# A gathered running sum times a matrix, on one core: gathers that convert to 16 bits as they land, in place of a cast on ScalarE

## The chip, the cores and the metric

The kernel runs on one core of a Trainium2 chip. The metric is the device time of one execution in microseconds (us). Three executions of the kernel before gave 450.98, 449.62 and 450.46 us, so the median is 450.46 us. One more execution was taken with the hardware profiler, and it is the one that the profile shows.

The core has five engines with a queue of instructions each: TensorE (PE in the profile, with its weight loads as PEld), VectorE (DVE), ScalarE (ACT), GpSimd (POOL) and SyncE (SP). They wait for one another through semaphores. Transfers between the chip's memory (DRAM) and the on-chip memory run on 16 DMA engines; here SyncE issues the stores and GpSimd the gathers.

## The reference

```python
B, S, N, D = 16, 4096, 2048, 512       # x: [B, S, D] float32, indices: [B, N] sorted, w: [D, D]
gathered = x[b_idx, indices, :].copy()  # [B, N, D]
cs = np.cumsum(gathered, axis=1)        # running sum over the N gathered rows
return np.matmul(cs, w).astype(np.float32)
```

Each of 16 batches picks 2048 of its 4096 rows of 512 floats, sums them up from the first to each row, and multiplies every running sum by one 512 x 512 matrix. 67 MB are read and 67 MB written.

## The kernel before, in words

The 32,768 gathered rows are cut into 256 tiles of 128 rows, 16 tiles to a batch; two neighbouring tiles make a pair (`R = 2`). Each tile goes through six steps.

1. **Gather** (GpSimd, L136): one indirect DMA fetches 128 rows of 2 KB, one per partition, into a tile of `g32`, a ring of 8 pairs in float32. From the 17th tile on, a gather waits on `s_c` until the tile that stood in its place in the ring has been cast.
2. **Cast** (ScalarE, L150): a copy from `g32` to `g16`, a ring of 8 pairs in float16. It waits for its gather (`s_g`).
3. **Sums** (TensorE, L162): four matmuls against a triangle of ones (`ut`, or `uq` in the first and last two pairs), which give the running sums within the tile, already transposed, in `pa` (four tiles of PSUM).
4. **Carry** (VectorE, L194; L181 in the first tile of a batch): adds the last sum of the tile before and writes float16 to `cst` (a ring of four pairs). Each carry waits for the sums (`s_a`) and for the carry before (`s_d`).
5. **Projection** (TensorE, L206): four matmuls of 512 columns against `w16` into `pb` (four tiles of PSUM). The two tiles of a pair are interleaved row by row, so a projection waits until both carries of its pair are done.
6. **Drain** (ScalarE, L218): a copy from `pb` to `ob`, four buffers of four tiles. SyncE stores 1 MB from each when its four drains are done (L236); the first eight pairs and the last four are stored one by one.

The order on each queue is written out by hand. On TensorE a list (L343 to L351) puts the sums of a tile `LEAD = 2` tiles ahead of the projections, so that the queue reads sums of tile u + 2, projection of tile u, and so on; a projection also needs a free place in `pb` (`s_e`, the drain of the tile four before), and sums need a free place in `pa` (`s_d`, the carry of the tile four before). On ScalarE the queue reads cast of tile u + 4, drain of tile u (`FAR = 4`). GpSimd's queue holds nothing but the 256 gathers after a short setup. TensorE, VectorE and ScalarE run the middle of the program as loops with 16 tiles to a pass.

`Lane.need` (L21) is the helper that emits a wait, and leaves it out where the engine has already waited for as much.

Of the kernel before, what the change touches and what calls it, by code (L numbers as in the profile page):

```python
# [7 lines left out]
P = 128  # L8
FP32 = mybir.dt.float32
FP16 = mybir.dt.float16  # L10
# [23 lines left out]
def kernel(  # L34
# [7 lines left out]
    nc = tc.nc  # L42

    B, S, D = x.shape
    N = indices.shape[1]
    R = 2
    Q = P // R
    DC = D // P
    NT = N // P
    T = B * NT  # L50
# [2 lines left out]
    KI = T // P  # L53
    FIRST = 2 * R
    NG = 16
    LEAD = 2
    FAR = 4
    NH = 8
    NA = 4
    NB = 4  # L60
    NC = 4
    W = 2
    NO = 4
    U = NT
    V = max(U, W * R * NO)
    assert U == NT == NG == W * R * NO and V % U == 0 and V % (W * R * NO) == 0 and T % V == 0 and U % NG == 0 and U % NA == 0 and U % (R * NC) == 0 and U % NB == 0
    assert D == 512 and N % (R * P) == 0 and T % P == 0

    x_flat = x.rearrange("b s d -> (b s) d")
# [1 line left out]
    const = ctx.enter_context(tc.tile_pool(name="const", bufs=1))  # L71
# [8 lines left out]
    ut = const.tile([P, R, Q], FP16)  # L80
    uq = const.tile([P, P], FP16)
    ident = const.tile([P, P], FP32)
    zeros = const.tile([P, D], FP16)
    spare = const.tile([P, 1], FP16)
    g32 = [const.tile([P, R, D], FP32, name=f"g32_{i}") for i in range(NG // R)]
    g16 = [const.tile([P, R, D], FP16, name=f"g16_{i}") for i in range(NH)]
    cst = [const.tile([P, DC, R, P], FP16, name=f"cst{i}") for i in range(NC)]
    ob = [const.tile([P, W, R, D], FP32, name=f"ob{i}") for i in range(NO)]
    pa = [ps.tile([P, DC, R, Q], FP32, name=f"pa{i}") for i in range(NA)]
# [4 lines left out]
    def sem(name):  # L94
        return tc.alloc_semaphore(name)

    s_z, s_ut, s_wc, s_if, s_pt, s_prep, s_c = (
        sem(f"s_{n}") for n in ("z", "ut", "wc", "if", "pt", "prep", "c")
    )
# [2 lines left out]
    s_idx = [sem(f"s_idx{k}") for k in range(KI)]  # L102
    s_f = [sem(f"s_f{i}") for i in range(NO)]
    s_ol = sem("s_ol")
    s_g = [sem(f"s_g{i}") for i in range(NG)]
    s_o = [sem(f"s_o{i}") for i in range(NO)]
    s_a = sem("s_a")
    s_d = sem("s_d")
    s_b = sem("s_b")
    s_e = sem("s_e")  # L110

    pool, pe, dve, act, sp = (
        Lane(e) for e in (nc.gpsimd, nc.tensor, nc.vector, nc.scalar, nc.sync)
    )

    casts = []
    done = 0
    for u in range(T):
        far = 2 if u < R else 3 if u < U // 2 or T - 1 - u < R * R else FAR
        casts.append(range(done, max(done, min(u + far + 1, T))))  # L120
        done = max(done, min(u + far + 1, T))

    for u in range(2 * U, T - 2 * U):
        assert casts[u] == range(u + FAR, u + FAR + 1)

    def gather(t):
        g, r = divmod(t, R)
        if t >= NG:
            pool.need(s_c, R * (g + 1) - NG)
        if t < FIRST:  # L130
            pool.need(s_first[g], 16)
            ap = idx_first[:, t, 0:1]
        else:
            pool.need(s_prep, t // P + 1)
            ap = idxg[:, t // P, t % P : t % P + 1]
        nc.gpsimd.indirect_dma_start(  # L136
            out=g32[g % (NG // R)][:, r, :],
            out_offset=None,
            in_=x_flat,
            in_offset=bass.IndirectOffsetOnAxis(ap=ap, axis=0),  # L140
            element_offset=(t // NT) * S * D,
        ).then_inc(s_g[t % NG], 16)


    PLAIN = (0, 1, G - 2, G - 1)

    def cast(t, first=None):
        g, r = divmod(t, R)
        act.need(s_g[t % NG], 16 * (t // NG + 1), first)
        nc.scalar.copy(  # L150
            out=g16[g % NH][:, r, :], in_=g32[g % (NG // R)][:, r, :]
        ).then_inc(s_c, 1)

    def sums(t, u, first=None):
        g, r = divmod(t, R)
        tiles = None if first is None else R * first
        pe.need(s_c, t + 1, tiles)
        pe.need(s_d, t - NA + 1, tiles)
        for c in range(DC):
            if c == 1 and u is not None:  # L160
                pe.need(s_e, u - NB + 1, tiles)
            mm = nc.tensor.matmul(  # L162
                out=pa[t % NA][:, c],
                lhsT=g16[g % NH][:, r, c * P : (c + 1) * P],
                rhs=uq[:] if first is None and g in PLAIN else ut[:],
                start=(c == 0),
                stop=(c == DC - 1),
            )
        mm.then_inc(s_a, 1)
# [28 lines left out]
    def project(u, t, first=None):  # L198
        g, j = divmod(u, R)
        tiles = None if first is None else R * first  # L200
        pe.need(s_e, u - NB + 1, tiles)
        pe.need(s_d, u + 1 if first is None and g in PLAIN else R * (g + 1), tiles)
        for c in range(DC):
            if c == 2 and t is not None:
                pe.need(s_d, t - NA + 1, tiles)
            mm = nc.tensor.matmul(  # L206
                out=pb[u % NB][:],
                lhsT=cst[g % NC][:, c, j, :],
                rhs=w16[:, c, :],
                start=(c == 0),  # L210
                stop=(c == DC - 1),
            )
        mm.then_inc(s_b, 1)

    def drain(u, first=None):
        g, j = divmod(u, R)
        act.need(s_b, u + 1, first)
        nc.scalar.copy(out=ob[g // W % NO][:, g % W, j], in_=pb[u % NB][:]).then_inc(s_e, 1)  # L218
# [22 lines left out]
    with nc.allow_non_contiguous_dma(reason="a few indices, one per partition"):  # L241
        for k, eng in enumerate((nc.sync, nc.scalar)):
            t = k * R
            eng.dma_start(
                out=idx_first[:, t : t + R, :],
                in_=indices[0, t * P : (t + R) * P]
# [4 lines left out]
    for k in range(KI):  # L251
        nc.sync.dma_start(
            out=idx64[:, k, :], in_=idx_rows[k * P : (k + 1) * P, :]
# [10 lines left out]
    for i in range(G // W - NO, G // W - 2):  # L264
# [8 lines left out]
        out=ident[:],  # L273
        in_=ident[:],
# [7 lines left out]
        out=ut[:],  # L282
        in_=ut[:],
# [9 lines left out]
        out=uq[:],  # L293
        in_=uq[:],
# [6 lines left out]
    for t in range(T):  # L301
        gather(t)
# [15 lines left out]
    for k in range(KI):  # L318
# [3 lines left out]
            out=pb[k % NB][:, :P], in_=idxf[:, k, :], identity=ident[:]  # L322
# [20 lines left out]
    order = []  # L343
    done = 0
    for u in range(T):
        lead = 1 if min(u, T - 1 - u) < R * R else min(LEAD, 2 + (u + 4) // 16, 2 + (T - 1 - u) // 15)
        first = u if u // R in PLAIN else u // R * R + R - 1
# [4 lines left out]

    head = order.index((False, 2 * U - 1)) + 1
    tail = order.index((False, T - 2 * U - 1)) + 1
    step = 2 * U
    for i in range(head + step, tail):
        assert order[i] == (order[i - step][0], order[i - step][1] + U)

    def run(i, first=None):
        is_sums, t = order[i]  # L360
        after = next((v for k, v in order[i + 1 :] if k != is_sums), None)
        if first is not None:
            t -= 2 * U
            after -= 2 * U
        if is_sums:
            sums(t, after, first)
        else:
            pe.need(s_wc, DC)
            project(t, after, first)

    for i in range(head):
        run(i)
    with nc.tensor.Fori(2 * U // R, (T - 2 * U) // R, U // R) as first:
        pe.new_pass()
        for i in range(head, head + step):
            run(i, first)
    for i in range(tail, len(order)):
        run(i)
# [7 lines left out]
    def step(u, first=None):  # L386
        if u % (W * R) == 0:
            i, slot = divmod(u // (W * R), NO)
            if first is None and i == 1:
                act.need(s_f[slot], 16 * (W - 1 + (slot == 0) * (R - 1)))  # L390
            act.need(s_o[slot], 16 * i, first)
        for t in casts[u if first is None else 2 * U + u]:
            cast(t if first is None else t - 2 * U, first)
        drain(u, first)


    for u in range(2 * U):
        step(u)
    with nc.scalar.Fori(2 * U, T - 2 * U, V) as first:
        act.new_pass()  # L400
        for u in range(V):
            step(u, first)
    for u in range(T - 2 * U, T):
        step(u)
# [30 lines left out]
```

## Time and profile before

| what | value |
|---|---|
| median of three executions | 450.46 us |
| the profiled execution, its own time | 447.37 us |
| its span, from the first to the last instruction | 445.6 us |
| TensorE busy | 324.6 us |
| ScalarE busy | 278.2 us, of it casts 159.8 us and drains 150.6 us, which overlap a little |
| GpSimd busy | 244.3 us in 266 instructions, 256 of them gathers |
| VectorE busy | 178.9 us |
| moved by the DMA engines | 135.69 MB, mean 304 GB/s |

Times are microseconds unless marked ns. "Busy" is the time in which an engine had an instruction at work. A wait is put down to the instruction that released it; "remote" stands where the profile knows none, and "issue" is time in which the engine waited for nothing that the profile shows. Matmuls are pipelined and their ends are modelled, so the end of a matmul in the record is not the moment at which its result was announced. In the timeline, each row is the start, the length, the engine, the line and what was done, and in brackets how long the engine had been idle and what released it.

### The profile page before, as it was taken

Reading aid. Unit: us, or ns where it says so; the run is one execution under the profiler, and the core shown is the slowest. Engines: PE = TensorE matmul, PEld = TensorE weight load, DVE = VectorE, ACT = ScalarE, POOL = GpSimd, SP = SyncE. Lnnn points to the kernel's source line nnn. Section 1 sums busy time; section 2 is a strip of 40 time slices with the busy share of each in tenths; the row PEclk is TensorE's granted clock in tenths of the full one; section 3 lists DMA queues with packets and bytes.
Section 4 is the critical chain, followed back from the end, with each engine's and each line's share of the span. In section 5 each row is a group of like instructions: output and inputs, shape, how many; then the busy total and the mean of one; then the engine's idle time right before and its main releaser. Section 6 shows DMA issues by size and latency. Waiting matters only on the chain.

```text
span 445.6 us, 6369 instructions
## 1 busy us (share of the span) xinstructions
PE 324.6 (73%) x2066; PEld 168.1 (38%) x2066; DVE 178.9 (40%) x263; ACT 278.2 (62%) x516; POOL 244.3 (55%) x266
## 2 busy tenths in 40 slices
PE   7508777777778856968669677777688677777795
PEld 3203343344334433434335333343344333333452
DVE  2104343434334334444344434344434444334562
ACT  4206575667666656767567656666766666566794
POOL 6754555555565555656556555565564555555500
PEclk9757898989898999898997999898996999998999
DMA  7866878988998998899998999888998898998976
GB/s 228 258 197 209 313 267 303 346 300 326 325 330 307 313 335 311 300 348 317 323 326 276 320 301 338 306 317 316 342 324 305 311 313 308 322 314 311 333 282 257
DMA packets 39947, 135.69 MB, mean 304 GB/s; under 512 B 5888, under 2 KB 6144, under 8 KB 39936
## 3 DMA queue, kind: packets, MB, share of 16 engines
q0 software_dynamic: 20480, 67.13, 45.3%
q1 hardware_dynamic: 18896, 67.90, 41.3%
q10 hardware_dynamic: 560, 0.53, 0.4%
q8 instruction: 5, 0.08, 0.1%
q14 instruction: 6, 0.05, 0.0%
HBM read 68.42 MB, written 67.11 MB: 304 GB/s over the span
## 4 chain that ended last, share of the span: by engine, by line
PE 73%; DVE 10%; another core or an unknown queue 7%; issue 5%; ACT 1%; DMA 1%; POOL 0%; DVEq 0%; SPq 0%
PE pb L206 51%; PE pa L162 22%; DVE cst L194 10%; DMA g<-in_x_dram,idx_first 1%; ACT g L150 1%; ACT ob L218 1%; DMA idx_first<-in_indices_dram 0%; POOL g L136 0%; DVE cst L181 0%; DVEq L26 0%; DVEq L333 0%; SPq L430 0%; SPq L92 0%
## 5 line engine op out<-in xcount | busy, mean ns | idle before, releaser
L206 PE MATMUL pb<-w,cst 128*128 128x512 f16 x1024 | 284.7, 404 | 99.9 <-DVE cst L194 91.0
L136 POOL DMA_INDIRECT g<-in_x_dram,idxg x252 | 238.8, 948 | 175.1 <-ACT g L150 105.5
L194 DVE TENSOR_TENSOR cst<-pa,cst 128x512 f16<-128x512 f32 x240 | 166.1, 692 | 239.9 <-PE pa L162 168.8
L218 ACT COPY ob<-pb 128x512 f32<-128x512 f32 x256 | 150.6, 588 | 157.2 <-PE pb L206 94.2
L150 ACT CAST g<-g 128x512 f16<-128x512 f32 x256 | 159.8, 625 | 0.5 <-DMA g<-in_x_dram,idx_first 0.4
L206 PEld LDWEIGHTS pb<-w,cst 128*128 128x128 f16 x1024 | 91.6, 102 | 180.2 <-DVE cst L194 100.1
L162 PE MATMUL pa<-ut,g 128*128 128x128 f16 x992 | 100.9, 227 | 13.8 <-issue 12.6
L162 PEld LDWEIGHTS pa<-ut,g 128*128 128x128 f16 x992 | 79.4, 102 | 83.1 <-issue 30.7
L181 DVE CAST cst<-pa 128x512 f16<-128x512 f32 x16 | 11.0, 690 | 14.4 <-PE pa L162 9.1
L309 PE MATMUL pb<-zeros 128*128 128x512 f16 x16 | 7.2, 632 | 1.5 <-DVE zeros L313 1.5
L136 POOL DMA_INDIRECT g<-in_x_dram,idx_first x4 | 4.0, 1003 | 1.6 <-issue 0.9
L309 PEld LDWEIGHTS pb<-zeros 128*128 128x128 f16 x16 | 2.3, 150 | 4.8 <-issue 3.3
L162 PEld LDWEIGHTS pa<-uq,g 128*128 128x128 f16 x32 | 2.7, 111 | 2.3 <-ACT g L150 0.6
L162 PE MATMUL pa<-uq,g 128*128 128x128 f16 x32 | 3.4, 243 | 0.1
L385 ACT CAST w<-w 128x512 f16<-128x512 f32 x2 | 1.1, 618 | 2.9 <-DMA w<-in_w_dram 2.9
L382 ACT ACT_TABLE_LOAD x1 | 1.3, 1283 | 2.5 <-issue 2.5
L316 DVE CAST idxf<-idx 128x128 f32<-128x128 uint32 x2 | 0.5, 227 | 4.5 <-DMA idx<-in_indices_dram 4.5
L321 PE MATMUL pb<-ident,idxf 128*128 128x128 f32 x2 | 0.9, 449 | 0.7 <-DVE idxf L316 0.7
L321 PEld LDWEIGHTS pb<-ident,idxf 128*128 128x128 f32 x2 | 0.4, 207 | 1.6 <-DVE idxf L316 1.4
L330 DVE CAST w<-w 128x512 f16<-128x512 f32 x2 | 0.8, 428 | 0.3 <-DMA w<-in_w_dram 0.3
L313 DVE MEMSET zeros<- 128x256 uint32 x1 | 0.3, 272 | 1.1 <-SPq L92 1.1
L327 DVE CAST idxg<-pb 128x128 uint32<-128x128 f32 x2 | 0.6, 288 | 0.4 <-PE pb L321 0.4
(11 smaller groups left out, 2.1 us busy)
## 6 DMA issues: line engine op xcount, KB each, us to landing
out_dram<-ob SPq DMA_DIRECT2D x58, 1024.0 KB
out_dram<-ob SPq DMA_DIRECT2D x10, 512.0 KB, 3.1
g<-in_x_dram,idxg POOLq DMA_INDIRECT x252
out_dram<-ob SPq DMA_DIRECT2D x4, 256.0 KB, 2.8
w<-in_w_dram ACTq DMA_DIRECT2D x2, 256.0 KB
w<-in_w_dram SPq DMA_DIRECT2D x2, 256.0 KB
idx<-in_indices_dram SPq DMA_DIRECT2D x2, 128.0 KB, 2.7
g<-in_x_dram,idx_first POOLq DMA_INDIRECT x4
```

What stands on the lines that cost most here:

```text
L136: nc.gpsimd.indirect_dma_start(out=g32[g % (NG // R)][:, r, :], out_offset=None, in_=x_flat, in_offset=bass.IndirectOffsetOnAxis(ap=ap, ax ...
L150: nc.scalar.copy(out=g16[g % NH][:, r, :], in_=g32[g % (NG // R)][:, r, :]).then_inc(s_c, 1)
L162: mm = nc.tensor.matmul(out=pa[t % NA][:, c], lhsT=g16[g % NH][:, r, c * P : (c + 1) * P], rhs=uq[:] if first is None and g in PLAIN else ...
L181: nc.vector.tensor_copy(out=dst, in_=src).then_inc(s_d, 1)
L194: nc.vector.tensor_tensor(out=dst, in0=src, in1=last, op=mybir.AluOpType.add).then_inc(s_d, 1)
L206: mm = nc.tensor.matmul(out=pb[u % NB][:], lhsT=cst[g % NC][:, c, j, :], rhs=w16[:, c, :], start=(c == 0), stop=(c == DC - 1),)
L218: nc.scalar.copy(out=ob[g // W % NO][:, g % W, j], in_=pb[u % NB][:]).then_inc(s_e, 1)
L309: nc.tensor.matmul(out=pb[NB - 1][:], lhsT=zeros[:, :P], rhs=zeros[:], start=True, stop=True)
L321: nc.tensor.transpose(out=pb[k % NB][:, :P], in_=idxf[:, k, :], identity=ident[:]).then_inc(s_pt, 1)
L330: nc.vector.tensor_copy(out=w16[:, c, :], in_=w32[:, c, :]).then_inc(s_wc, 1)
L382: nc.scalar.copy(out=spare[:], in_=zeros[:, :1])
L385: nc.scalar.copy(out=w16[:, c, :], in_=w32[:, c, :]).then_inc(s_wc, 1)
```

## The change

The ring `g32` and the cast are gone. A gather now writes float16 straight into `g16`, so the DMA converts the rows on their way. The ring is as long as before, 8 pairs. What used to wait for the cast now waits elsewhere: the sums wait for the gather itself (`s_g`, now 32 semaphores in place of 16), and a gather waits for the sums (`s_a`).

That last wait is made once for a pair. For tiles 0 to 15 the pair may be issued when its second tile is at most 8 tiles ahead of the sums that are done. The limit is 10 tiles for tiles 16 to 23, 12 and 14 for the next two eights, and 16, which is the length of the ring, from tile 40 on.

`LEAD` goes from 2 to 4: the sums run four tiles ahead of the projections in the middle of the program, with two and then three at the start and the same backwards at the end. TensorE's loop has 32 tiles to a pass in place of 16. Stores, drains and carries are as they were.

```diff
-    NG = 16
-    LEAD = 2
-    FAR = 4
-    NH = 8
+    NG = 16
+    NS = 32
+    FREE = 2
+    LEAD = 4
...
-    g32 = [const.tile([P, R, D], FP32, name=f"g32_{i}") for i in range(NG // R)]
-    g16 = [const.tile([P, R, D], FP16, name=f"g16_{i}") for i in range(NH)]
+    g16 = [const.tile([P, R, D], FP16, name=f"g16_{i}") for i in range(NG // R)]
...
     def gather(t):
         g, r = divmod(t, R)
-        if t >= NG:
-            pool.need(s_c, R * (g + 1) - NG)
+        if t % FREE == 0:
+            pool.need(s_a, t + FREE - min(NG, 3 * R + max(t // (4 * R), 1) * R))
...
         nc.gpsimd.indirect_dma_start(
-            out=g32[g % (NG // R)][:, r, :],
+            out=g16[g % (NG // R)][:, r, :],
...
-        ).then_inc(s_g[t % NG], 16)
+        ).then_inc(s_g[t % NS], 16)
...
-    def cast(t, first=None):
-        g, r = divmod(t, R)
-        act.need(s_g[t % NG], 16 * (t // NG + 1), first)
-        nc.scalar.copy(
-            out=g16[g % NH][:, r, :], in_=g32[g % (NG // R)][:, r, :]
-        ).then_inc(s_c, 1)
...
     def sums(t, u, first=None):
-        pe.need(s_c, t + 1, tiles)
-        pe.need(s_d, t - NA + 1, tiles)
+        skip = 0 if first is None else 2 * U
+        pe.need(s_g[t % NS], 16 * (t // NS + 1) - skip // R, first)
+        pe.need(s_d, t - NA + 1 - skip, tiles)
...
-    with nc.tensor.Fori(2 * U // R, (T - 2 * U) // R, U // R) as first:
+    with nc.tensor.Fori(2 * U // R, (T - 2 * U) // R, V // R) as first:
...
-        for t in casts[u if first is None else 2 * U + u]:
-            cast(t if first is None else t - 2 * U, first)
         drain(u, first)
```

Three places show how the queues read. The first is TensorE at the start of its loop, in the kernel before. The number behind `pa` and `pb` is the tile's, modulo 4; the one behind `cst` is the pair's, modulo 4, and the one behind `g16` the pair's, modulo 8.

```order
L162 MATMUL pa2_98<-ut_67,g16_1_81 128x128 [waits s_d]
...
L206 MATMUL pb0_100<-w16_66,cst0_88 128x512 [waits s_d]
L206 MATMUL pb0_100<-w16_66,cst0_88 128x512 x3
...
L162 MATMUL pa3_99<-ut_67,g16_1_81 128x128 [waits s_c]
...
L162 MATMUL pa3_99<-ut_67,g16_1_81 128x128 [waits s_e]
L162 MATMUL pa3_99<-ut_67,g16_1_81 128x128 x2
L206 MATMUL pb1_101<-w16_66,cst0_88 128x512 x4
```

The same place in the changed kernel:

```order
L145 MATMUL pa0_88<-ut_67,g16_2_74 128x128 [waits s_d]
...
L190 MATMUL pb0_92<-w16_66,cst0_80 128x512 [waits s_d]
L190 MATMUL pb0_92<-w16_66,cst0_80 128x512 x3
L145 MATMUL pa1_89<-ut_67,g16_2_74 128x128 [waits s_g5]
...
L145 MATMUL pa1_89<-ut_67,g16_2_74 128x128 [waits s_e]
L145 MATMUL pa1_89<-ut_67,g16_2_74 128x128 x2
L190 MATMUL pb1_93<-w16_66,cst0_80 128x512 x2
```

Between the sums and the projection that stands behind them there was one pair (`g16_1`, tiles 34 and 35, before `cst0`, tiles 32 and 33), and there are now two (`g16_2`, tiles 36 and 37). The wait for the cast, `s_c`, has become one for the gather itself.

The second place is GpSimd's queue from the fifth gather on. Before, it ran up to the sixteenth tile without a wait:

```order
L136 DMA g32_3_75<-in_x_dram,idxg_64 128x512 x2
L136 DMA g32_4_76<-in_x_dram,idxg_64 128x512 x2
L136 DMA g32_5_77<-in_x_dram,idxg_64 128x512 x2
L136 DMA g32_6_78<-in_x_dram,idxg_64 128x512 x2
L136 DMA g32_7_79<-in_x_dram,idxg_64 128x512 x2
L136 DMA g32_0_72<-in_x_dram,idxg_64 128x512 [waits s_c]
```

Now it waits for the sums from the ninth tile on, once for a pair:

```order
L125 DMA g16_3_75<-in_x_dram,idxg_64 128x512 x2
L125 DMA g16_4_76<-in_x_dram,idxg_64 128x512 [waits s_a]
L125 DMA g16_4_76<-in_x_dram,idxg_64 128x512
L125 DMA g16_5_77<-in_x_dram,idxg_64 128x512 [waits s_a]
L125 DMA g16_5_77<-in_x_dram,idxg_64 128x512
```

So eight gathers stand ahead of the first wait for a compute engine, where there were sixteen.

The third place is ScalarE, in the unrolled start. Before, a cast stood ahead of each drain:

```order
L150 CAST g16_4_84<-g32_4_76 128x512 [waits s_g8]
L218 COPY ob1_93<-pb0_100 128x512 [waits s_b]
L150 CAST g16_4_84<-g32_4_76 128x512 [waits s_g9]
L218 COPY ob1_93<-pb1_101 128x512 [waits s_b]
L150 CAST g16_5_85<-g32_5_77 128x512 [waits s_g10]
```

Now the queue holds the drains alone:

```order
L202 COPY ob1_85<-pb0_92 128x512 [waits s_b]
L202 COPY ob1_85<-pb1_93 128x512 [waits s_b]
L202 COPY ob1_85<-pb2_94 128x512 [waits s_b]
L202 COPY ob1_85<-pb3_95 128x512 [waits s_b]
L202 COPY ob2_86<-pb0_92 128x512 [waits s_b]
```

The wait for the gather, which was ScalarE's, has gone to TensorE's sums with the cast.

More of the change, by code (lines that the diff above doesn't have):

```diff
@@ L64 @@
     U = NT
-    V = max(U, W * R * NO)
-    assert U == NT == NG == W * R * NO and V % U == 0 and V % (W * R * NO) == 0 and T % V == 0 and U % NG == 0 and U % NA == 0 and U % (R * NC) == 0 and U % NB == 0
+    V = NS
+    assert U == W * R * NO and V % NS == 0 and NS % NG == 0 and FREE == R and NS == 16 * R and 2 * U % NS == 0 and (T - 4 * U) % V == 0 and U % (W * R * NO) == 0 and U % NA == 0 and U % (R * NC) == 0 and U % NB == 0
     assert D == 512 and N % (R * P) == 0 and T % P == 0
@@ L104 @@
     s_ol = sem("s_ol")
-    s_g = [sem(f"s_g{i}") for i in range(NG)]
+    s_g = [sem(f"s_g{i}") for i in range(NS)]
     s_o = [sem(f"s_o{i}") for i in range(NO)]
@@ L114 @@
     )
[L116 to L124, printed above, removed]
     def gather(t):
         g, r = divmod(t, R)
-        if t >= NG:
-            pool.need(s_c, R * (g + 1) - NG)
+        if t % FREE == 0:
+            pool.need(s_a, t + FREE - min(NG, 3 * R + max(t // (4 * R), 1) * R))
         if t < FIRST:
@@ L156, in sums @@
         tiles = None if first is None else R * first
-        pe.need(s_c, t + 1, tiles)
-        pe.need(s_d, t - NA + 1, tiles)
+        skip = 0 if first is None else 2 * U
+        pe.need(s_g[t % NS], 16 * (t // NS + 1) - skip // R, first)
+        pe.need(s_d, t - NA + 1 - skip, tiles)
         for c in range(DC):
             if c == 1 and u is not None:
-                pe.need(s_e, u - NB + 1, tiles)
+                pe.need(s_e, u - NB + 1 - skip, tiles)
             mm = nc.tensor.matmul(
                 out=pa[t % NA][:, c],
-                lhsT=g16[g % NH][:, r, c * P : (c + 1) * P],
-                rhs=uq[:] if first is None and g in PLAIN else ut[:],
+                lhsT=g16[g % (NG // R)][:, r, c * P : (c + 1) * P],
+                rhs=uq[:] if g in PLAIN else ut[:],
                 start=(c == 0),
@@ L200, in project @@
         tiles = None if first is None else R * first
-        pe.need(s_e, u - NB + 1, tiles)
-        pe.need(s_d, u + 1 if first is None and g in PLAIN else R * (g + 1), tiles)
+        skip = 0 if first is None else 2 * U
+        pe.need(s_e, u - NB + 1 - skip, tiles)
+        pe.need(s_d, (u + 1 if g in PLAIN else R * (g + 1)) - skip, tiles)
         for c in range(DC):
             if c == 2 and t is not None:
-                pe.need(s_d, t - NA + 1, tiles)
+                pe.need(s_d, t - NA + 1 - skip, tiles)
             mm = nc.tensor.matmul(
@@ L354 @@
     tail = order.index((False, T - 2 * U - 1)) + 1
-    step = 2 * U
+    step = 2 * V
     for i in range(head + step, tail):
-        assert order[i] == (order[i - step][0], order[i - step][1] + U)
+        assert order[i] == (order[i - step][0], order[i - step][1] + V)
     def run(i, first=None):
@@ L361, in run @@
         after = next((v for k, v in order[i + 1 :] if k != is_sums), None)
-        if first is not None:
-            t -= 2 * U
-            after -= 2 * U
         if is_sums:
@@ L398 @@
         step(u)
-    with nc.scalar.Fori(2 * U, T - 2 * U, V) as first:
+    with nc.scalar.Fori(2 * U, T - 2 * U, U) as first:
         act.new_pass()
-        for u in range(V):
+        for u in range(U):
             step(u, first)
```

## The prediction

> **What bounds the kernel now.** I read the page first, then the waits of the even middle (60 to 420 us), then one stretch of the timeline, then the start.
>
> ```profile
> span 445.6 us, 6369 instructions
> PE 324.6 (73%) x2066; PEld 168.1 (38%) x2066; DVE 178.9 (40%) x263; ACT 278.2 (62%) x516; POOL 244.3 (55%) x266
> ...
> q0 software_dynamic: 20480, 67.13, 45.3%
> q1 hardware_dynamic: 18896, 67.90, 41.3%
> q10 hardware_dynamic: 560, 0.53, 0.4%
> ```
>
> No engine is busy for more than 73%. The 16 DMA engines are: gathers (q0) take 45.3% of their time and stores (q1) 41.3%, 86.6% in all. The middle, by windows:
>
> ```profile
> 20.00:40.00 20.00, 7.31 (x34) 3.24 (x33) 3.46 (x5) 4.55 (x9) 10.15 (x11) 0.55 0.64 196
> 40.00:60.00 20.00, 16.29 (x104) 8.26 (x104) 7.51 (x11) 13.30 (x25) 12.92 (x14) 0.91 0.90 311
> ...
> 60.00:420.00 360.00, 267.32 (x1738) 140.06 (x1737) 151.34 (x219) 233.59 (x436) 205.18 (x218) 0.94 0.90 316
> ```
>
> The columns are busy time and count on PE, PEld, DVE, ACT and POOL, then TensorE's clock, the DMA share and GB/s. In 360 us VectorE does 219 carries: 360 / 219 = 1.64 us a tile. The waits in it (total, times, longest):
>
> ```profile
> DVE cst L194 <- PE pa L162: 142.3, 123, 3.6
> POOL g L136 <- ACT g L150: 94.3, 49, 2.9
> ...
> ACT ob L218 <- PE pb L206: 84.2, 81, 3.2
> PE pb L206 <- DVE cst L194: 77.0, 47, 3.2
> ```
>
> It is a ring: TensorE waits for carries, VectorE and ScalarE for TensorE, GpSimd for casts. Casts do not wait for gathers, so gathers are early enough. Where the ring stops is seen at 274 to 281 us:
>
> ```profile
> 273.86 0.95 POOL L136 DMA_INDIRECT g<-in_x_dram,idxg  x1 [0.36 <-issue]
> ...
> 274.68 1.03 PE L206 MATMUL pb<-w,cst 128*128 128x512 f16 x4
> ...
> 275.11 0.94 POOL L136 DMA_INDIRECT g<-in_x_dram,idxg  x1 [0.30 <-issue]
> ...
> 275.55 0.39 PE L162 MATMUL pa<-ut,g 128*128 128x128 f16 x4
> ...
> 275.75 0.59 ACT L218 COPY ob<-pb 128x512 f32<-128x512 f32 x1
> 275.77 1.03 PE L206 MATMUL pb<-w,cst 128*128 128x512 f16 x4
> ...
> 276.36 0.95 POOL L136 DMA_INDIRECT g<-in_x_dram,idxg  x1 [0.30 <-issue]
> ...
> 276.86 1.03 PE L206 MATMUL pb<-w,cst 128*128 128x512 f16 x4
> ...
> 277.62 0.95 POOL L136 DMA_INDIRECT g<-in_x_dram,idxg  x1 [0.31 <-issue]
> ...
> 277.82 0.69 DVE L194 TENSOR_TENSOR cst<-pa,cst 128x512 f16<-128x512 f32 x1 [2.24 <-PE pa L162]
> 279.97 0.59 ACT L218 COPY ob<-pb 128x512 f32<-128x512 f32 x1 [3.12 <-remote]
> 280.03 1.49 DVE L194 TENSOR_TENSOR cst<-pa,cst 128x512 f16<-128x512 f32 x2 [1.51 <-remote]
> ...
> 280.77 1.89 PE L206 MATMUL pb<-w,cst 128*128 128x512 f16 x4 [2.67 <-DVE cst L194]
> ...
> 281.34 0.95 POOL L136 DMA_INDIRECT g<-in_x_dram,idxg  x1 [2.77 <-ACT g L150]
> ```
>
> Undisturbed, TensorE does a tile every 276.86 - 275.77 = 1.09 us. The projection of 274.68 is drained at 275.75, at once; that of 275.77 should be over at 276.80 and is drained at 279.97, and the sums of 275.55 are taken up at 277.82, 1.9 us late, by a VectorE that had been idle for 2.24. So TensorE's results are announced late, and what stands beside the lateness is a run of four gathers without a pause, 1.25 us apart (0.95 at work and 0.30 between). It ends 2.4 us after the last began. GpSimd then waits for casts, the backlog moves, and the next run begins. I take the run as the cause, since the start shows the same at a larger scale:
>
> ```profile
> 29.75 0.94 POOL L136 DMA_INDIRECT g<-in_x_dram,idxg  x1 [0.30 <-issue]
> 31.55 0.69 DVE L194 TENSOR_TENSOR cst<-pa,cst 128x512 f16<-128x512 f32 x1 [11.92 <-remote]
> 34.38 0.59 ACT L218 COPY ob<-pb 128x512 f32<-128x512 f32 x1 [8.72 <-remote]
> ...
> 35.18 1.03 PE L206 MATMUL pb<-w,cst 128*128 128x512 f16 x2 [8.87 <-DVE cst L194]
> ```
>
> Gathers run without a pause until 29.75 + 0.94 us, and VectorE sits idle for 11.92 us.
>
> **The change part by part.**
>
> *The first gathers.* Eight in place of sixteen stand ahead of the first wait, so the long run ends 8 x 1.25 = 10 us earlier. What the run costs: from 20 to 60 us TensorE issues 34 + 104 = 138 matmuls, 17 tiles at 8 each, where 40 / 1.64 gives 24: 7 tiles, 11.5 us. Bounds: 0 (the hold-up comes in portions instead) to 11.5. I take 10, since the length of the run is what went with the wait.
>
> *The lead.* A projection waits for carries 47 times in the middle, 77.0 us in all, 1.64 on the mean and 3.2 at most. Two more tiles of sums in hand are 2 x 1.09 = 2.2 us of projections during a hold-up. `pb` and `pa` allow it: they have four places each, and at the start of a hold-up the drains are up to date. Most waits are shorter than 2.2 us, so of the 77.0 us some 65 could go. That is the upper end; the lower is 0, if drains, held up by the same late announcements, become the wait (the 84.2 us of ScalarE).
>
> *The cap.* Less waiting means denser transfers, and there the room is small:
>
> ```profile
> GB/s 228 258 197 209 313 267 303 346 300 326 325 330 307 313 335 311 300 348 317 323 326 276 320 301 338 306 317 316 342 324 305 311 313 308 322 314 311 333 282 257
> ```
>
> The densest slice has 348 GB/s, the middle 316. At 348 the middle would take 360 x 316 / 348 = 327 us, 33 less. I take 33 for lead and casts together.
>
> *The casts.*
>
> ```profile
> L136 POOL DMA_INDIRECT g<-in_x_dram,idxg x252 | 238.8, 948 | 175.1 <-ACT g L150 105.5 <-issue 69.6
> ...
> L218 ACT COPY ob<-pb 128x512 f32<-128x512 f32 x256 | 150.6, 588 | 157.2 <-PE pb L206 94.2 <-remote 51.0 <-issue 11.8
> L150 ACT CAST g<-g 128x512 f16<-128x512 f32 x256 | 159.8, 625 | 0.5 <-DMA g<-in_x_dram,idx_first 0.4
> ```
>
> 159.8 us of ScalarE go, at nothing on the path: cast and drain together are about 0.62 + 0.59 = 1.21 us a tile at most, under the 1.64, and ScalarE waits for projections beside it. Without them a backlog of drains clears at 0.59 each; that helps the lead to its 65 and is under the same cap.
>
> *The gathers' own price.* No transfer of this trace converts, so this is the open term. On GpSimd: the nearest row is the gather at 948 ns, with 0.30 between 1.25 us, and 256 x 1.25 = 320 us of 445.6. On ScalarE the converting copy is 625 against 588 ns, 6% more: 1.32 us for a gather would still be under 1.64. On the DMA engines, the lower end is a gain, since half the bytes are written on chip. For the upper end, a row of 1 KB at the target may stop two source rows from sharing a packet. The q10 row is the nearest: 0.53 MB in 0.4% of 16 x 445.6 = 7130 us, 28.5 us, is 18.6 GB/s on an engine, against 67.90 MB in 41.3%, 23.1 GB/s, of the stores: 1.24 times the time for a byte. I take no extra cost, which is nearest to the gather's own row: it reads the same rows from the same place.
>
> The Trainium skill ("Perfetto Trace Analysis", DMA Optimizations) says that transfers under 2 KB carry a significant overhead each, which speaks against this change. The gathers here already move 2 KB rows at 67.13 MB in 45.3%, 20.8 GB/s on an engine, so the trace shows no more than a tenth between them and the stores; no run here has 1 KB rows, and by the rule the sum would be the first rival's.
>
> *The waits.* A sum now waits for its own gather in place of a cast that waited for it. The limit of 14 to 16 tiles is over 20 us of work at 1.64, and casts four tiles ahead never waited, so this costs nothing; at the start, 8 tiles are 13 us. Queued behind a sum that waits are the projections of all later tiles; behind a gather that waits for the sums, only gathers. GpSimd's wait passes from casts (94.3 us) to sums, one step nearer to TensorE. The loop of 32 tiles halves the number of passes; its cost lies under matmuls.
>
> **The sum.** 445.6 - 10 - 33 = 402.6 us of span. The median of the runs lies 450.46 - 445.6 = 4.9 above it: 407.5 us; I say 407.
>
> **The rivals.**
>
> *The DMA engines take longer over a converting row* (slower). Place: q0. At 1.24 times, 45.3 x 1.24 + 41.3 = 97.5% of 445.6, 434 us of work for each engine; at the middle's share of 0.90 the span is 483, the median 488. At 1.5 times, 109% or 487 us, and 541 of span. At 0.90 each percent on q0 is 2.2 us, and 43 of gains are used up at about 1.2 times, from which it decides. The same result comes if GpSimd takes longer to write a converting gather, from 1.64 / 1.25 = 1.3 times; at twice, 256 x 2.5 = 640. For: no row shows the price, and the engines are at 0.90 already. Against: the bytes read are the same and those written on chip fewer.
>
> *The hold-ups stay as they are.* Gathers now follow the sums directly, so each release brings the next run sooner, and four places of `pb` and `pa` stop TensorE as before. Only the start is won: 450.5 - 10 = 440. For: the ring is made of the same announcements, 142.3 us of VectorE's waiting. Against: the 2.67 us of the stretch shown needed two tiles.
>
> *The change does not do what it says*, the gains of start and lead cancelled by a small price of conversion: about 450.
>
> **How the numbers follow.** The forecast, 385 to 428, gets 0.52; the hold-ups that stay, 428 to 449, 0.13; no change, 0.04; the dearer gather, 452 to 640, 0.31, half of it under 500. The range is 385 to 500: it leaves out the far half of the dear gather and a little below. The forecast's own is 385 to 428, its lower end with more than half of the lead's 65 in place of 33. About 0.3% is what a measurement of this kernel can tell from no change: faster 0.64, same 0.05, slower 0.31.
>
> **What would show it.** Right: the start's VectorE wait of 11.92 us is gone and 20 to 60 us hold over 20 tiles; projections wait for carries under 40 us in the middle; q0 near or under 45% x 445.6 = 202 us, and gathers at about 948 ns. Wrong: q0's time over 240 us, or gathers over 1.3 us each, with sums waiting for gathers; or runs of gathers still followed by carries 2 us late at the same 1.64 us a tile.

## The result and the profile after

| | before | changed |
|---|---|---|
| median | 450.04 us (4 runs) | 409.09 us (4 runs) |
| span of the profiled execution | 445.6 us | 406.9 us |
| ratio | | 0.909, 95% interval 0.906 to 0.912 |

407 us had been forecast. The page of the changed kernel:

```profile
span 406.9 us, 6043 instructions
PE 319.7 (79%) x2066; PEld 161.0 (40%) x2066; DVE 178.4 (44%) x263; ACT 143.2 (35%) x260; POOL 242.6 (60%) x266
...
q0 software_dynamic: 36864, 33.57, 57.2%
q1 hardware_dynamic: 18896, 67.90, 42.9%
...
L125 POOL DMA_INDIRECT g<-in_x_dram,idxg x252 | 237.1, 941 | 139.1 <-issue 56.1
```

GpSimd needs as long for a converting gather as for a plain one (941 ns, before 948). The DMA engines need longer: 57.2% of 406.9 us is 233 us, against 45.3% of 445.6, 202 us, with half the bytes on the target's side. There are 36,864 packets in place of 20,480, 16,384 more, which is one more for every second of the 32,768 rows: two rows no longer share a packet.

The windows (busy time and count on PE, PEld, DVE, ACT and POOL, then clock, DMA share, GB/s) and the waits of the middle, 60 to 380 us:

```profile
20.00:60.00 40.00, 28.40 (x160) 14.29 (x161) 15.23 (x23) 11.44 (x20) 25.95 (x28) 0.83 0.92 201
...
60.00:380.00 320.00, 258.69 (x1702) 130.21 (x1700) 145.67 (x212) 114.99 (x212) 200.04 (x214) 0.97 1.04 260
```

```profile
ACT ob L202 <- PE pb L190: 163.6, 92, 3.7
DVE cst L177 <- PE pa L145: 130.8, 66, 3.6
POOL g L125 <- issue: 46.3, 152, 0.3
POOL g L125 <- PE pa L145: 37.8, 41, 2.2
...
POOL g L125 <- remote: 36.2, 21, 1.9
...
PE pb L190 <- issue: 23.2, 21, 2.2
PE pb L190 <- DVE cst L177: 17.2, 18, 1.5
```

In the middle a tile takes 320 / 212 = 1.51 us where it took 1.64: 0.13 us for each of some 224 tiles is 30 us of the 38.7 that the span lost. From 20 to 60 us TensorE did 160 matmuls where, counted in one window as here, it did 136: 3 tiles or 4.9 us. The rest lies in the first 20 us and the end.

Two rows say where the 0.13 us are. TensorE waits less ahead of its projections: 17.2 us are put down to carries, before 77.0 in 360. Part of that is only a change of name, since the row of projections that wait for "issue" grew from 8.0 to 23.2 us; together it is 40 us where it was 85. But VectorE still waits up to 3.6 us for sums, so the late announcements are still there. What became shorter is GpSimd's idle time: (46.3 + 37.8 + 36.2) / 214 = 0.56 us for each gather, where (60.8 + 94.3) / 218 = 0.71 stood before (the 60.8 us are its "issue" row in the middle of the kernel before, shown here with the row for casts):

```profile
POOL g L136 <- ACT g L150: 94.3, 49, 2.9
...
POOL g L136 <- issue: 60.8, 169, 1.3
```

That the two rows go together proves nothing yet, since all engines wait in one ring. So the experiments undid or moved one step each.

### The profile page after: what moved, and what is told of

It is laid out like the page before. It is cut to its first block, busy times and chain, and to the rows that moved or that the text cites. A ratio compares the mean times of both kernels' runs of the same rounds, so it can differ in the third digit from the quotient of the medians.

```text
span 406.9 us, 6043 instructions
## 1 busy us (share of the span) xinstructions
PE 319.7 (79%) x2066; PEld 161.0 (40%) x2066; DVE 178.4 (44%) x263; ACT 143.2 (35%) x260; POOL 242.6 (60%) x266
## 3 DMA queue, kind: packets, MB, share of 16 engines
q0 software_dynamic: 36864, 33.57, 57.2%
## 4 chain that ended last, share of the span: by engine, by line
PE 75%; issue 11%; DVE 8%; another core or an unknown queue 4%; DMA 2%; ACT 0%; DVEq 0%; SPq 0%
PE pb L190 54%; PE pa L145 20%; DVE cst L177 7%; DMA g<-in_x_dram,idx_first 1%; DMA idx_first<-in_indices_dram 0%; DVE cst L164 0%; ACT ob L202 0%; DVEq L26 0%; SPq L409 0%; SPq L91 0%
## 5 line engine op out<-in xcount | busy, mean ns | idle before, releaser
L190 PE MATMUL pb<-w,cst 128*128 128x512 f16 x1024 | 281.3, 395 | 61.4 <-DVE cst L177 31.6
L202 ACT COPY ob<-pb 128x512 f32<-128x512 f32 x256 | 140.6, 592 | 254.0 <-PE pb L190 192.2
L190 PEld LDWEIGHTS pb<-w,cst 128*128 128x128 f16 x1024 | 87.9, 101 | 143.1 <-DVE cst L177 44.4
L145 PE MATMUL pa<-ut,g 128*128 128x128 f16 x992 | 105.6, 224 | 17.3 <-issue 15.0
L145 PEld LDWEIGHTS pa<-ut,g 128*128 128x128 f16 x992 | 76.7, 100 | 88.7 <-issue 37.4
L293 PE MATMUL pb<-zeros 128*128 128x512 f16 x16 | 5.1, 477 | 1.5 <-DVE zeros L297 1.5
```

The lines of the kernel that those rows point to most:

```text
L145: mm = nc.tensor.matmul(out=pa[t % NA][:, c], lhsT=g16[g % (NG // R)][:, r, c * P : (c + 1) * P], rhs=uq[:] if g in PLAIN else ut[:], star ...
L190: mm = nc.tensor.matmul(out=pb[u % NB][:], lhsT=cst[g % NC][:, c, j, :], rhs=w16[:, c, :], start=(c == 0), stop=(c == DC - 1),)
L293: nc.tensor.matmul(out=pb[NB - 1][:], lhsT=zeros[:, :P], rhs=zeros[:], start=True, stop=True)
```

## The experiments

The kernels of each of the four sections below ran on one chip, beside the kernel before on that chip, and are compared with it. That proved needful: on the first section's chip the kernel before took 348.72 us, on the other three chips 449.6 to 450.8. I call them the quick chip and the slow chips.

### Four edits on a quick chip

Theory one was the prediction's: TensorE's announcements come late while gathers run without a pause, and the lead of four tiles and the shorter first run cover that. Theory two: the cast, once out of the ring of waits, is the gain.

The changed kernel with the old lead:

```diff
-    LEAD = 4
+    LEAD = 2
```

> The changed kernel with the sums two tiles ahead of the projections in place of four; all else as changed. First theory (late announcements during runs of gathers are covered by the lead): most of what the middle won is lost again, 420 to 437 us, and projections wait for carries more than 60 us in all. Second theory (what counts is that the cast left ScalarE's queue and the ring of waits): no change, 407 to 411 us.

The changed kernel without the limit at the start:

```diff
-            pool.need(s_a, t + FREE - min(NG, 3 * R + max(t // (4 * R), 1) * R))
+            pool.need(s_a, t + FREE - NG)
```

> The changed kernel without the tighter limit at the start: a pair of gathers waits only until the ring of 16 tiles has room. First theory: 16 gathers run without a pause again, TensorE's results are announced late until they end, and the start costs 7 to 10 us more, 415 to 420 us. Second theory: the start was paid for by the casts, so no change, 407 to 411 us.

The kernel before with the longer lead:

```diff
-    LEAD = 2
-    FAR = 4
+    LEAD = 4
+    FAR = 6
```

> The kernel before with its casts and plain gathers, but the sums four tiles ahead of the projections and the casts six ahead. First theory: the lead covers the hold-ups whatever the gathers convert, 415 to 430 us. Second theory: casts stay in the ring, 447 to 453 us.

The kernel before with the limit at the start added:

```diff
             pool.need(s_c, R * (g + 1) - NG)
+        if t < 40 and r == 0:
+            pool.need(s_a, t + R - min(NG, 3 * R + max(t // (4 * R), 1) * R))
```

> The kernel before with the tighter limit of the changed kernel on its first 40 gathers, which then also wait for the sums; all else as before. First theory: the long run of gathers at the start is cut, and 7 to 10 us go, 440 to 443 us. Second theory: no change, 448 to 452 us.

Measured, with the kernel before at 348.72 us: changed with a lead of two 353.48 us (ratio 1.014, 1.011 to 1.016), changed without the limit 354.28 (1.016, 1.014 to 1.018), before with a lead of four 350.53 (1.005, 1.003 to 1.007), before with the limit 349.06 (1.001, 1.000 to 1.002). None of the numbers expected for either theory was met, since none was for such a chip. The last kernel's page, its queues and its waits over the whole span show what is different:

```profile
GB/s 234 245 347 373 373 370 409 413 415 408 411 416 415 415 415 415 414 414 415 414 413 410 410 412 415 414 412 416 414 413 411 410 414 412 413 409 414 399 285 188
...
q0 software_dynamic: 20480, 67.13, 50.0%
q1 hardware_dynamic: 18896, 67.90, 48.3%
```

```profile
DVE cst L196 <- PE pa L164: 145.4, 238, 1.9
...
POOL g L138 <- issue: 66.4, 218, 0.3
...
ACT g L152 <- DMA g<-in_x_dram,idxg: 51.8, 163, 1.5
```

Casts wait for gathers here, 51.8 us in all; in the kernel before on a slow chip it was 0.5. GpSimd's row for "issue", 0.3 us at most 218 times, says that gathers follow one another almost without a pause, and yet VectorE's longest wait is 1.9 us: announcements come in time. The DMA engines move some 413 GB/s and fall behind: a gather issued between 60 and 120 us lands after 8.4 us (median), one issued between 260 and 320 us after 14.8. So I take them to bind, with GpSimd's 1.25 us a gather close behind. There the converting gathers cost engine time: 58.8% of 352.8 us for q0 in the kernel without the limit is 207 us, against 50.0% of 347.5, 174 us, here, 1.19 times, and both converting kernels are 1.4 to 1.6% slower than the kernel before. That the conversion is the reason is not isolated, since a gather in them also waits for the sums in place of the cast. The changed kernel itself did not run on this chip.

### Lead and bytes on a slow chip

> The changed kernel as it is, once more, beside the kernel before on the same chip. First theory, as the last runs amended it (the change pays by covering late announcements, and a chip on which they come in time is bound by its DMA engines): on a chip where the kernel before takes about 450 us, 409; where it takes about 349, 351 to 356, since a converting gather keeps the DMA engines 15 to 20% longer. Second theory (the cast in the ring is what costs): 9% less on every chip, 317 us on the quick one.

> The kernel before with casts and plain gathers, the sums four tiles ahead and the casts six. First theory: where the kernel before takes 450 us, 415 to 435; where it takes 349, no gain, 348 to 351. Second theory: 447 to 453 us on the slow chip.

> The changed kernel with the sums two tiles ahead. First theory: where the kernel before takes 450 us, 420 to 437; where it takes 349, the same as the changed kernel within 2 us. Second theory: the same as the changed kernel on every chip.

The fourth kernel fetches half rows:

```diff
-    x_flat = x.rearrange("b s d -> (b s) d")
+    x_half = x.rearrange("b s (h d) -> (b s h) d", h=2)
...
-            out=g16[g % (NG // R)][:, r, :],
+            out=g16[g % (NG // R)][:, r, 0 : D // 2],
...
-                lhsT=g16[g % (NG // R)][:, r, c * P : (c + 1) * P],
+                lhsT=g16[g % (NG // R)][:, r, c % 2 * P : (c % 2 + 1) * P],
```

> The changed kernel with gathers of half a row: as many instructions and as many rows, each of 256 floats in place of 512, read from other places than the indices mean; the sums use the first two quarters of a tile twice. So its result is not the reference's, and all engines but the DMA engines do the same work. If the late announcements follow the number of gathers, a slow chip still shows them and gains less than 20 us over 409; if they follow the bytes, 360 to 380 us there. Where the DMA engines bind (349 us), the time falls to what GpSimd's 256 gathers at 1.25 us need, 330 to 340 us.

Measured, with the kernel before at 450.83 us: changed 408.78 us (0.910, 0.902 to 0.918); changed with a lead of two 409.70; half rows 409.56 (two runs; 0.911, 0.901 to 0.921); before with a lead of four 443.25 (0.985, 0.976 to 0.994).

The changed kernel's gain is the same again. The lead is worth 0.9 us in it, with ranges that overlap (408.63 to 409.99, and 409.08 to 410.26), where 11 to 28 had been expected: theory one falls in this part. In the kernel before it is worth some 7 us, well short of the range. Bytes are worth nothing on a slow chip; the page with half rows shows a third less DMA time (36.5% against 57.2%) and the same lateness:

```profile
q0 software_dynamic: 36864, 16.79, 36.5%
...
DVE cst L177 <- PE pa L145: 132.0, 66, 3.7
```

With a lead of two the timeline repeats itself, and so one cycle shows the pace:

```profile
299.81 0.94 POOL L125 DMA_INDIRECT g<-in_x_dram,idxg  x1 [1.33 <-PE pa L145]
...
301.06 0.94 POOL L125 DMA_INDIRECT g<-in_x_dram,idxg  x1 [0.30 <-issue]
...
302.30 0.94 POOL L125 DMA_INDIRECT g<-in_x_dram,idxg  x1 [0.30 <-issue]
...
303.54 0.94 POOL L125 DMA_INDIRECT g<-in_x_dram,idxg  x1 [0.31 <-issue]
...
305.57 1.49 DVE L177 TENSOR_TENSOR cst<-pa,cst 128x512 f16<-128x512 f32 x2 [2.17 <-PE pa L145]
305.63 0.59 ACT L202 COPY ob<-pb 128x512 f32<-128x512 f32 x1 [0.91 <-PE pb L190]
305.81 0.94 POOL L125 DMA_INDIRECT g<-in_x_dram,idxg  x1 [1.33 <-PE pa L145]
```

Four gathers 1.25 us apart, a held announcement that comes 2.0 us after the last one began (305.57), and 0.24 us later the next run: 6.00 us for four tiles, 1.50 each. The pace is GpSimd's, and TensorE's lead does not enter. The changed kernel itself, with its lead of four, mostly issues six gathers in a run (23 of its 44 runs from 60 to 380 us), at the same pace.

In the stretch of the prediction the run was not of four gathers but of six. It began before the rows shown there, and the cast that released the next run is not among them either:

```profile
271.30 0.95 POOL L136 DMA_INDIRECT g<-in_x_dram,idxg  x1 [2.79 <-ACT g L150]
...
272.55 0.95 POOL L136 DMA_INDIRECT g<-in_x_dram,idxg  x1 [0.30 <-issue]
...
280.45 0.62 ACT L150 CAST g<-g 128x512 f16<-128x512 f32 x1
```

The last of the six begins at 277.62. The announcement follows at 280.03, then a drain and this cast, and the next run at 281.34, 1.31 us later. The cycle is 281.34 - 271.30 = 10.04 us for six tiles, 1.67 each; without 1.31 - 0.24 = 1.07 us of it, six tiles would take 1.50 each, the pace found here. That is a third theory: on a slow chip a cycle is the run, the late announcement, and what stands between it and the next gather. Before, ScalarE stood there; now nothing does.

### What stands between, and how many gathers

The kernel before, casts, plain gathers and all, with one semaphore changed:

```diff
         if t >= NG:
-            pool.need(s_c, R * (g + 1) - NG)
+            pool.need(s_a, R * (g + 1) - NG)
```

> The kernel before with its casts and plain gathers, but a gather waits for the sums of the tile 16 before (s_a, TensorE's own announcement) in place of that tile's cast (s_c); nothing else is changed. Third theory (on the slow chip the pace is GpSimd's: a run of gathers, the late announcement after it, and what stands between that announcement and the next gather, which was drain and cast and is now nothing): 408 to 420 us where the kernel before takes 450. Where it takes 349, no change. If the conversion itself or the freed ScalarE is what pays, 445 to 452 us on the slow chip.

And the changed kernel with half the gathers:

```diff
-    for t in range(T):
+    for t in range(0, T, R):
         gather(t)
...
-        pe.need(s_g[t % NS], 16 * (t // NS + 1) - skip // R, first)
+        pe.need(s_g[(t - r) % NS], 16 * (t // NS + 1) - skip // R, first)
...
-                lhsT=g16[g % (NG // R)][:, r, c * P : (c + 1) * P],
+                lhsT=g16[g % (NG // R)][:, 0, c * P : (c + 1) * P],
```

> The changed kernel with half the gathers: only even tiles are gathered, whole rows, and the sums of an odd tile use the even tile's rows once more, so its result is not the reference's. It gathers as many bytes as the kernel with half rows (409.6 us on the slow chip) in half as many instructions. If the number of gathers sets the pace there, 300 to 340 us; if their number does not matter either, 400 to 410. Where the kernel before takes 349, 300 to 320 us, which is TensorE's own 1.09 us a tile and the ends.

Measured, with the kernel before at 450.52 us: the one semaphore gives 413.50 us (0.918, 0.913 to 0.923), half the gathers 296.31 (0.658, 0.653 to 0.663), just under the 300 to 340 expected.

So the wait alone brings 37 us, nearly all of the change, with 256 casts still on ScalarE and no conversion. Its timeline has the cycle of the changed kernel with a lead of two, 307.37 - 301.38 = 5.99 us for four tiles, with 0.24 us from the announcement to the gather:

```profile
301.38 0.94 POOL L136 DMA_INDIRECT g<-in_x_dram,idxg  x1 [1.30 <-PE pa L162]
...
305.13 0.95 POOL L136 DMA_INDIRECT g<-in_x_dram,idxg  x1 [0.30 <-issue]
...
307.13 1.49 DVE L194 TENSOR_TENSOR cst<-pa,cst 128x512 f16<-128x512 f32 x2 [2.16 <-PE pa L162]
307.37 0.94 POOL L136 DMA_INDIRECT g<-in_x_dram,idxg  x1 [1.29 <-PE pa L162]
```

It is not this stretch alone. From 60 to 380 us GpSimd's mean wait for sums is 71.4 / 54 = 1.32 us, with 213 / 54 = 3.9 gathers to a wait; for casts it was 94.3 / 49 = 1.92 us, with 218 / 49 = 4.4:

```profile
POOL g L136 <- PE pa L162: 71.4, 54, 1.7
```

Half the gathers move as many bytes as the half rows, 33.57 / 2 MB, and take 113 us less, on two chips whose kernel before differs by 0.3 us. Lateness goes with the number of gathers and not with bytes:

```profile
q0 software_dynamic: 18432, 16.79, 40.5%
...
DVE cst L177 <- PE pa L145: 74.4, 182, 1.3
```

The longest wait of VectorE for sums is 1.3 us, where it was 3.6, and its waits come to 74.4 us of the 234 from 60 us to the end, where they were 130.8 us of 320. Whether instructions, rows or packets count is not separated, nor is the pause: GpSimd waits here before nearly every gather, so that there are no runs any more.

### The start, and ScalarE put back

The kernel of the one semaphore, with the limit at the start as well:

```diff
-        if t >= NG:
-            pool.need(s_c, R * (g + 1) - NG)
+        if r == 0:
+            pool.need(s_a, t + R - min(NG, 3 * R + max(t // (4 * R), 1) * R))
```

> The kernel before with its casts and plain gathers, gathers waiting for the sums as in the changed kernel, the tighter limit at the start included; sums two tiles ahead. Third theory: what is left between 413.5 and the changed kernel's 409 is the start, so 405 to 411 us where the kernel before takes 450; where it takes 349, 347 to 351, which would be at least as quick as either kernel on each chip. If the conversion is worth something of its own, 412 to 416 on the slow chip.

The changed kernel with a drain put between announcement and gather:

```diff
-            pool.need(s_a, t + FREE - min(NG, 3 * R + max(t // (4 * R), 1) * R))
+            pool.need(s_e if t >= 3 * NG else s_a, t + FREE - min(NG, 3 * R + max(t // (4 * R), 1) * R))
```

> The changed kernel, but from the 49th tile on a gather waits for the drain (s_e) of the tile 16 before in place of its sums, so that ScalarE stands again between TensorE's announcement and the next gather, with a drain and no cast. Third theory: the cycle of four gathers, 6.0 us, grows by the drain's 0.59 us and by what the drain comes later than the sums, 425 to 445 us where the kernel before takes 450. If the cast itself was what cost, 407 to 412 us. Where it takes 349, 351 to 356.

Measured, with the kernel before at 449.55 us: 411.74 us (0.915, 0.912 to 0.918) and 419.35 us (0.933, 0.929 to 0.937).

The limit at the start is worth less than 2 us where 2.5 to 8.5 had been expected: 0.915 lies inside the interval of 0.918 without it. The changed kernel's 0.909 to 0.910 stays a little ahead, by about 2 us, which the runs do not split among conversion, lead and ScalarE's relief. The drain put back costs 10 us of the 41, with no cast in the queue; the direction is the third theory's, the size below its range of 16 to 36. (A drain also comes after its projection, so more than the drain stands between.) GpSimd's waits are for ScalarE again:

```profile
POOL g L125 <- ACT ob L202: 71.0, 41, 5.4
```

So the wait is shown to carry the gain, but why it does is shown only in part: 30 us stay gained with ScalarE between announcement and gather. What the cast adds to the drain is not measured alone. Nor is one more difference: a tile's sums need its cast, so the wait for the sums is the later of the two, and it lets GpSimd run less far ahead. The old wait with a shorter reach was not run.

No kernel that ran is shown to beat both. The one semaphore in the kernel before takes 413.5 us on a slow chip, and it keeps plain gathers, which were the cheaper ones on the quick chip, but it did not run there.

## Why the prediction was right, and what in it was wrong

The time, the direction and the place of the hold-ups were right; the terms behind the time were not. The sum had 10 us for the first gathers, 33 for lead and casts and nothing for the wait; the runs show under 2, about 1, and 37. That the time agrees is luck. Of the signs, VectorE's wait of 11.92 us at the start is gone (the longest there is 4.29) and gathers take 941 ns, but q0 takes 233 us where 202 had been named. Carries still come late, at 1.51 us a tile.

**Late announcements beside runs of gathers: right.** They are still there after the change, they go (3.6 us at most becomes 1.3) when half the gathers go, and bytes do not matter. What was argued from one stretch, whose run was taken for four gathers and has six, is now shown for the number of gathers. That it holds on each chip was taken for granted and is wrong: on the quick chip gathers run almost without a pause and nothing is late.

**"The first gathers", 10 us: too much.** The first 60 us did gain some 7, but the limit alone brought less than 2 us between two kernels that differ in it alone. TensorE's matmuls of the first 60 us tell where the rest comes from: 186 before, 208 with the one semaphore, 223 with the limit too, 222 in the changed kernel. More than half of the gain at the start is the new wait's.

**"The lead", up to 65 us, with the cap 33: wrong.** TensorE's waits ahead of projections did shrink, as forecast, and it brought 0.9 us. The step that failed was to price a wait of the busiest engine as if that engine set the pace. With a lead of two TensorE waits nearly as long as before, 19.1 + 60.5 = 80 us in 320, and the time is the same, since the cycle is GpSimd's. (The same wait of 1.48 us ahead of a projection is put down to the carry at 300.33 us and to "issue" at 306.32.)

```profile
PE pb L190 <- issue: 60.5, 40, 2.7
...
PE pb L190 <- DVE cst L177: 19.1, 12, 2.7
```

In the kernel before the longer lead, with casts six ahead, did bring 7.6 us.

**"The cap", 348 GB/s: no cap.** The densest slice of one run is what that run asked for. With the one semaphore a slow chip moves 347 GB/s on the mean of 60 to 380 us, with slices up to 362, and the quick chip 408 to 416 slice after slice. The changed kernel moves 260 there, so the agreement of the 33 us with the 30 of the middle is chance.

**"The casts", nothing on the path, and "the waits", costing nothing: wrong, and this is the term that carried the gain.** The prediction noted that GpSimd's wait passes from casts to sums, "one step nearer to TensorE", and gave it no price. Worked out from the stretch, 1.31 us from announcement to gather became 0.24, 1.07 us for six tiles, which is an estimate of 40 us for the 224 tiles of the middle. The one semaphore measures 37 us.

**"The gathers' own price", none: wrong, within its bounds.** GpSimd's part was right (941 ns). On the DMA engines it is 233 against 202 us, 1.15 times, and 1.19 on the quick chip, under the upper end of 1.24. On a slow chip it was hidden: with half rows q0's share falls to 36.5% and nothing is gained. On the quick chip, where the engines bind, converting kernels were 1.4 to 1.6% slower, which fits the first rival's mechanism at a small price. The Trainium skill ("Perfetto Trace Analysis", DMA Optimizations) says that transfers under 2 KB carry a significant overhead each; the trace agrees as far as the target's side counts, with 1 KB there, 2 KB still at the source, and 15% more engine time for the same rows.

**The second rival**, hold-ups that stay as they are, described the mechanism better than the forecast did: they stayed, and each release brings the next run sooner. Its time, 440 us, was wrong, since it gave that nothing.

What stays open: what holds TensorE's announcements up, and why on some chips only. Whether it belongs to the chip or to what ran beside it then was not tried. One more number differs: the plain gathers took 202 us of the DMA engines' time on a slow chip and 174 on the quick one.

## What to carry to other kernels

In a ring of waits, price the step that a wait passes through and not only the engine that waits most: follow one cycle of the timeline from a release to the next instruction of the engine that closes the ring. Before paying for a large rewrite, try its new wait alone in the old kernel; here that was one semaphore and nine tenths of the gain. Compare on the same chip, and on more than one, before a gain is believed. Add a wait's "issue" and "remote" rows to the one with a name before two kernels are compared by it.

## What the runs showed of the hardware

- The same program took 348.7 us on one chip and 450 on others, with a granted clock of 0.98 to 1.00 there and 0.90 to 0.93 here. The clock does not explain it: with the one semaphore it was 0.97 on a slow chip, at 413.5 us, and with half the gathers 1.00.
- On the slow chips VectorE waited up to 3.6 us for TensorE's announcements beside gathers issued every 1.25 us, and 1.3 us at most with half as many gathers; halving the bytes of each changed nothing (409.56 us against 408.78).
- A gather that converts float32 rows of 2 KB to float16 is issued as fast as a plain one, but takes 1.15 to 1.19 times the DMA engines' time, in 36,864 packets where there were 20,480.
- The DMA share of a window can exceed 1 (1.04 in the middle of the changed kernel): the times of an engine's packets overlap, so a share of 0.90 was no measure of the room that was left.
